# Two-layer pooling/attention decoder trunk on one core: in the feed-forward blocks, the low part of every second weight chunk comes from an accumulating DMA

## The chip, the cores and the metric

The kernel runs on one core of one Trainium2 chip. The metric is the device time of one execution in microseconds (us); lower is better. The kernel before takes 1941.47 us, the median of two runs (1940.99 and 1941.94 us).

A core has TensorE (PE, with its weight loads listed as PEld), VectorE (DVE), ScalarE (ACT), GpSimd (POOL) and SyncE (SP). Each runs its own instructions in the order in which they stand, and they wait for one another through semaphores. SP, ACT and POOL can issue DMAs, which 16 DMA engines carry out.

## The reference

All tensors are float32, for one sequence of 256 tokens with 2048 features. Two layers, each a token mixer and a SwiGLU feed-forward block with 5632 hidden features, each behind an RMS norm and with a residual add:

```
def swiglu(h, wg, wu, wd):
    return (jax.nn.silu(h @ wg) * (h @ wu)) @ wd

for i in range(DEPTH):                      # DEPTH = 2
    hn = rmsnorm(h, norm_mix[i])
    mix = pool_mixer(...) if i % 2 == 0 else diff_attention(...)
    h = h + mix
    h = h + swiglu(rmsnorm(h, norm_ffn[i]), w_gate[i], w_up[i], w_down[i])
return rmsnorm(h, final_norm)
```

`w_gate` and `w_up` are [2048, 5632], `w_down` is [5632, 2048]. The pool mixer of layer 0 multiplies four channel groups by [512, 512] weights and takes causal trailing means; layer 1 is differential attention with `w_qkv` [2048, 6144] and `w_o` [2048, 2048].

## The kernel before

**Three products for one.** A float32 product is carried by float32r operands, which hold 12 significant bits. A weight is split exactly into `wh + wl` and an activation into `xh + xl`. Activations stand feature-major, [128 features, 256 tokens], with `xh` and `xl` side by side. For one *unit*, a [128, 128] block of weights, TensorE runs two matmuls: `big` (line 95) streams [xh | xl], 512 columns, through `wh`, and `small` (line 98) streams `xh`, 256 columns, through `wl`. Both add into one PSUM tile `acc`.

**Chunks.** Weights are read in *chunks* of 8 units, [128, 1024] float32 or 512 KB, by `Stream.unit` (lines 76 to 87). For each chunk SP issues a load into `raw`, ACT copies `raw` to `whi` (the copy rounds, so this is `wh`), and DVE subtracts, `wlo = raw - whi`. `raw`, `whi` and `wlo` have four buffers each, so a chunk can be prepared at most four chunks ahead: the copy into `whi` waits until TensorE is through with the chunk four before.

**The feed-forward block** (lines 270 to 309). Gate and up: 44 output tiles each, in turns, gate 0, up 0, gate 1, up 1 and so on. One output tile has 16 units, two chunks, the first even and the second odd in its stream. Behind each, ACT copies one half of the PSUM tile (`g_c` or `u_c`, line 176), DVE adds the other half and scales, ACT takes the `silu` (line 284) or makes the high part of `h` (line 290). Down: 16 output tiles of 44 units, five and a half chunks each; behind each come two residual adds on DVE (lines 136 and 137, the tile `x_all`), then on ACT the square `sq` (line 131) and the next operand's high part `xg` (line 123). Over both layers the feed-forward has 528 chunks, 352 in gate and up and 176 in down; the other products have 134.

**What sets the order.** A tile framework's scheduler lays out each engine's instructions ahead of time, and so the preparation of a chunk stands about four chunks ahead of its use in the program of ACT, DVE and SP. After that the order on each engine is fixed. POOL does nothing after the start.

Of the kernel before, what the change touches and what calls it, by code (L numbers as in the profile page):

```python
# [17 lines left out]
S = 256  # L18
# [7 lines left out]
CU = 8  # L26
# [10 lines left out]
def trunk_kernel(ctx, tc, x_t, gains, subln, lam_in, band, dist,  # L37
                 pool_w, w_qk, w_v, w_o, w_gate, w_up, w_down, out):
    """Activations are kept feature-major ([feature, token]), so that every product takes
    weights as the stationary operand. A float32 product is carried by three float32r passes:  # L40
    w = wh + wl and x = xh + xl exactly, 12 significant bits each; [xh | xl] stream through wh
    into the halves of one PSUM bank, and xh through wl onto the first half. The norms' row
    scale is applied to the products, which lets them start before it is known."""
    nc = tc.nc
# [8 lines left out]

# [1 line left out]
    gain_sb = const.tile([P, 6, NK], F32, name="gain_sb")  # L55
# [14 lines left out]

# [1 line left out]
    class Stream:  # L72
        def __init__(self, w):
            self.w, self.next, self.have = w, 0, {}

        def unit(self, u):
            c = u // CU
            if c not in self.have:
                raw = wraw.tile([P, CU * P], F32, name="raw")
                nc.sync.dma_start(out=raw, in_=self.w[c])  # L80
                hi = whl.tile([P, CU * P], F32R, name="whi")
                lo = whl.tile([P, CU * P], F32R, name="wlo")
                nc.scalar.copy(hi, raw)  # L83
                nc.vector.tensor_tensor(lo, raw, f32(hi), ALU.subtract)  # L84
                self.have = {c: (hi, lo)}
            hi, lo = self.have[c]
            return hi, lo, (u % CU) * P

    def product(stream, u0, acts):
        """One output tile: units u0.. of the stream against acts; a bank [left | right]."""  # L90
        ps = acc_ps.tile([P, 2, S], F32, name="acc")
        n = len(acts)
        for k, a in enumerate(acts):
            hi, lo, at = stream.unit(u0 + k)
            big = lambda: nc.tensor.matmul(  # L95
                ps.rearrange("p a s -> p (a s)"), hi[:, at:at + P],
                a.rearrange("p a s -> p (a s)"), start=(k == 0), stop=(k == n - 1))
            small = lambda: nc.tensor.matmul(  # L98
                ps[:, 0, :], lo[:, at:at + P], a[:, 0, :], start=False, stop=False)
            if k < n - 1:  # L100
                big()
                small()
            else:
                small()
                big()
        return ps

    def rsqrt(ss, n, cols):
        """(ss / n + eps) ** -0.5 of [128, cols] sums, with one Newton step behind the
        square root's table."""  # L110
        v, s, t, r = (tmp.tile([P, 8], F32, name=f"rs_{x}") for x in "vstr")
        v, s, t, r = v[:, :cols], s[:, :cols], t[:, :cols], r[:, :cols]
        nc.vector.tensor_scalar(v, ss, 1.0 / n, EPS, ALU.mult, ALU.add)
        nc.scalar.activation(s, v, AF.Sqrt)
        nc.vector.reciprocal(s, s)
        nc.vector.tensor_tensor(t, s, s, ALU.mult)
        nc.vector.scalar_tensor_tensor(t, t, -0.5, v, ALU.mult, ALU.mult)
        nc.vector.scalar_tensor_tensor(r, t, 1.5, s, ALU.add, ALU.mult)
        return r

    def split(dst, src, gain):
        """dst = [hi | lo] of src * gain (gain by partition)."""
        nc.scalar.activation(dst[:, 0, :], src, AF.Copy, scale=gain)
# [15 lines left out]
    def token_product(stream, u0, acts):  # L139
        """[tokens, 512] in two banks: acts stationary against 512 columns of the stream."""  # L140
        ps = [acc_ps.tile([P, 512], F32, name="acc") for _ in range(2)]
# [10 lines left out]
    def norm_scale(ssq, rows=True):  # L152
        """Each token's rsqrt(mean square): by partition [128, 2], and [128, S] on every one."""
        ps = aux_ps.tile([P, 512], F32, name="aux")
# [18 lines left out]
    def join(ps, name):  # L173
        """left + right halves of a bank, in SBUF."""
        c = tmp.tile([P, S], F32, name=f"{name}_c", tag="join_c")
# [4 lines left out]

# [1 line left out]
    with tc.tile_pool(name="start", bufs=1, reuse_waits="tile") as st:  # L182
        band_sb = st.tile([P, 4, P + HALO + P], F32, name="band_sb")
        pool_stream = Stream(pool_w)
        nc.scalar.dma_start(out=gain_sb, in_=gains)
        # loads the activation table, and keeps TensorE's clock up, before the data is there
        warm = tmp.tile([P, 8], F32, name="warm")
# [7 lines left out]

        # the first groups' products in plain float32, which wait for no split
        zp = [None] * 4
# [72 lines left out]
    def ffn(layer, ssq, next_gain):  # L270
        """x += swiglu(rmsnorm(x)); prepares the next block's operand and squares."""
        gs, us, ds = Stream(w_gate[layer]), Stream(w_up[layer]), Stream(w_down[layer])
        ssq_next = tmp.tile([P, S], F32, name="ssq")
        with tc.tile_pool(name=f"ffn{layer}", bufs=1, reuse_waits="tile") as hp:
# [17 lines left out]
            for j in range(NK):  # L292
                if j == NK - 1:
                    # has the square root's table in place by the end of the products
                    pre = tmp.tile([P, 8], F32, name="warm")
# [16 lines left out]

# [1 line left out]
    ssq_next = tmp.tile([P, S], F32, name="ssq")  # L314
    with tc.tile_pool(name="attn", bufs=1, reuse_waits="tile") as ap_, \
# [7 lines left out]
        def transpose_probs(h, probs):  # L323
            """aT[h] = [keys, queries] by block of keys."""
            a_t = ap_.tile([P, 2, S], F32, name=f"aT{h}")
# [10 lines left out]
        for h in range(H):  # L336
            # q0 q1 k0 k1
            qk = ap_.tile([P, 4, S], F32, name=f"qk{h}", tag="qk", bufs=8)
            for i in range(4):
# [3 lines left out]
                if r is None:  # L343
# [4 lines left out]
                    nc.vector.tensor_scalar(qs_col, col, QK_SCALE, None, ALU.mult)  # L348
                    # lambda, on all partitions
                    lp = ap_.tile([P, 2], F32, name="lp")  # L350
# [80 lines left out]

# [1 line left out]
    _, r = norm_scale(ssq)  # L433
# [9 lines left out]
def _chunks(w):  # L443
    """[128, columns] -> [chunk, 128, CU * 128], so that each load reads one block of memory."""
    return w.reshape(P, -1, CU * P).transpose(1, 0, 2)


def _units(w):
    """[K, N] -> chunks of [128, N/128 * K/128 * 128]: by column tile, then by row tile."""
    K, N = w.shape  # L450
# [3 lines left out]
def _constants():  # L454
    """What the shapes alone give: the means' bands over tokens, and the distances."""
    import numpy as np
# [57 lines left out]
```

## Time and profile before

| | before |
|---|---|
| median of two runs | 1941.47 us |
| span of the profiled execution | 1939.9 us |
| PE busy | 1923.3 us, 99% |
| DVE busy | 1187.4 us, 61% |
| ACT busy | 938.8 us, 48% |
| POOL busy | 0.7 us |
| share of the span in which the 16 DMA engines carry the SP queue's packets | 59.4% |
| read from HBM | 350.96 MB |
| mean granted TensorE clock | 0.996 |

The span runs from the first to the last instruction; no separate device time of the profiled execution is listed, and the runs' median lies 1.6 us above the span. Matmuls are pipelined, so PE's busy time says that PE had always something to do, not that each matmul is as short as can be. The chain that ended last, followed back from the end, names the work that set the time. In a group of instructions, "idle before" is how long the engine waited ahead of them, and the arrow names what ended that wait.

### The profile page before, as it was taken

The page shows a single profiled execution, that of the slowest core. Times are in us where ns is not written, and L with a number is a line of the kernel's source. Part 1 is how long each engine was busy: PE and PEld are TensorE (multiplying, and loading weights), DVE is VectorE, ACT ScalarE, POOL GpSimd, SP SyncE. Part 2 cuts the span into 40 slices and gives each one's busy share as a digit, 9 for nine tenths or more (in the row PEclk, how much of TensorE's full clock was granted, in tenths as well). Part 3 has the DMA queues.
Part 4 walks back from the last instruction along what each step waited for, and adds up shares of the span by engine and source line. Part 5 has one row for each costly group of instructions (what it writes and reads, how often), then busy time and mean ns, then how long its engine had stood idle before and what let it go on. Part 6 is the DMA issues. An engine that isn't in the chain of part 4 may idle for free.

```text
span 1939.9 us, 27612 instructions
## 1 busy us (share of the span) xinstructions
PE 1923.3 (99%) x10786; PEld 1664.6 (86%) x10786; DVE 1187.4 (61%) x1722; ACT 938.8 (48%) x1379; POOL 0.7 (0%) x6
## 2 busy tenths in 40 slices
PE   9999999999999999999999999999999999999997
PEld 7888888888888888888888888888888888888886
DVE  7766666666655555666655676666666666555554
ACT  7544444454444444544455545454544445444442
POOL 0000000000000000000000000000000000000000
PEclk9999999999999999999999999999999999999999
DMA  6666666656666665555555466665666665666663
GB/s 203 193 186 187 189 184 190 185 184 188 186 190 185 189 190 187 174 174 174 175 178 168 160 188 182 188 185 186 185 189 183 190 187 185 187 190 188 186 188 115
DMA packets 99330, 354.86 MB, mean 183 GB/s; under 512 B 11264, under 2 KB 13568, under 8 KB 99200
## 3 DMA queue, kind: packets, MB, share of 16 engines
q1 hardware_dynamic: 97984, 352.01, 59.4%
q8 instruction: 84, 1.38, 0.3%
q10 hardware_dynamic: 1216, 1.10, 0.2%
q14 instruction: 46, 0.38, 0.1%
HBM read 350.96 MB, written 2.10 MB: 182 GB/s over the span
## 4 chain that ended last, share of the span: by engine, by line
PE 98%; DVE 1%; ACT 0%; DMA 0%; issue 0%; SPq 0%; DVEq 0%
PE acc L95 60%; PE acc L98 30%; PE acc L148 2%; PE acc L149 2%; PE acc L147 2%; PE aux L376 1%; DMA x_all<-x_t 0%; PE aux L419 0%; PE aux L252 0%; DVE y_out L437 0%; PE aux L405 0%; PE aux L251 0%; DVE wlo L84 0%; PE aux L406 0%; PE aux L407 0%; ACT sq_in L227 0%
## 5 line engine op out<-in xcount | busy, mean ns | idle before, releaser
L95 PE MATMUL acc<-xg,whi 128*128 128x512 f32 x3328 | 1164.3, 399 | 0.0
L84 DVE TENSOR_TENSOR wlo<-raw,whi 128x1024 fp32r<-128x1024 f32 x662 | 810.1, 1224 | 475.0 <-ACT whi L83 459.4
L83 ACT CAST whi<-raw 128x1024 fp32r<-128x1024 f32 x662 | 694.7, 1050 | 506.6 <-PE acc L95 436.9
L98 PE MATMUL acc<-xg,wlo 128*128 128x256 f32 x3328 | 902.4, 281 | 0.0
L95 PEld LDWEIGHTS acc<-xg,whi 128*128 128x128 f32 x3328 | 612.6, 188 | 134.2
L98 PEld LDWEIGHTS acc<-xg,wlo 128*128 128x128 f32 x3328 | 628.3, 189 | 20.0
L95 PE MATMUL acc<-h,whi 128*128 128x512 f32 x1408 | 492.1, 394 | 0.0
L98 PE MATMUL acc<-h,wlo 128*128 128x256 f32 x1408 | 390.5, 281 | 0.0
L95 PEld LDWEIGHTS acc<-h,whi 128*128 128x128 f32 x1408 | 262.6, 188 | 59.6
L98 PEld LDWEIGHTS acc<-h,wlo 128*128 128x128 f32 x1408 | 264.0, 188 | 2.9
L176 ACT COPY g_c<-acc 128x256 f32<-128x256 f32 x88 | 32.7, 372 | 166.8 <-PE acc L95 166.8
L176 ACT COPY u_c<-acc 128x256 f32<-128x256 f32 x88 | 32.7, 372 | 166.4 <-PE acc L95 166.4
L178 DVE TENSOR_TENSOR u_s<-acc,u_c 128x256 f32<-128x256 f32 x88 | 37.3, 424 | 92.0 <-ACT u_c L176 92.0
L178 DVE TENSOR_TENSOR g_s<-acc,g_c 128x256 f32<-128x256 f32 x88 | 37.3, 424 | 90.0 <-ACT g_c L176 90.0
L95 PE MATMUL acc<-oT,whi 128*128 128x512 f32 x256 | 89.2, 396 | 0.0
L98 PE MATMUL acc<-oT,wlo 128*128 128x256 f32 x256 | 69.1, 282 | 0.0
L147 PE MATMUL acc<-whi,xg 128*128 128x512 f32 x152 | 60.5, 400 | 2.6 <-ACT whi L83 2.6
L148 PE MATMUL acc<-wlo,xg 128*128 128x512 f32 x152 | 61.7, 406 | 0.7 <-DVE wlo L84 0.7
L149 PE MATMUL acc<-whi,xg 128*128 128x512 f32 x152 | 61.0, 401 | 0.0
L95 PEld LDWEIGHTS acc<-oT,whi 128*128 128x128 f32 x256 | 47.1, 188 | 9.9
L290 ACT CAST h<-h 128x256 fp32r<-128x256 f32 x88 | 35.8, 407 | 39.6 <-DVE h L289 39.6
L98 PEld LDWEIGHTS acc<-oT,wlo 128*128 128x128 f32 x256 | 48.1, 188 | 1.5
(109 smaller groups left out, 751.6 us busy)
## 6 DMA issues: line engine op xcount, KB each, us to landing
raw<-w_gate SPq DMA_DIRECT2D x176, 512.0 KB, 4.1
raw<-w_up SPq DMA_DIRECT2D x176, 512.0 KB, 3.7
raw<-w_down SPq DMA_DIRECT2D x176, 512.0 KB, 4.3
raw<-w_qk SPq DMA_DIRECT2D x64, 512.0 KB, 3.6
raw<-w_v SPq DMA_DIRECT2D x32, 512.0 KB, 3.6
raw<-w_o SPq DMA_DIRECT2D x32, 512.0 KB, 4.3
raw<-pool_w SPq DMA_DIRECT2D x6, 512.0 KB, 7.0
x_all<-x_t SPq DMA_DIRECT2D x3, 512.0 KB, 7.5
```

The lines of the kernel that those rows point to most:

```text
L83: nc.scalar.copy(hi, raw)
L84: nc.vector.tensor_tensor(lo, raw, f32(hi), ALU.subtract)
L95: big = lambda: nc.tensor.matmul(ps.rearrange("p a s -> p (a s)"), hi[:, at:at + P], a.rearrange("p a s -> p (a s)"), start=(k == 0), stop ...
L98: small = lambda: nc.tensor.matmul(ps[:, 0, :], lo[:, at:at + P], a[:, 0, :], start=False, stop=False)
L147: nc.tensor.matmul(ps[t], xh, hi[:, at:at + 512], start=(k == 0), stop=False)
L148: nc.tensor.matmul(ps[t], xh, lo[:, at:at + 512], start=False, stop=False)
L149: nc.tensor.matmul(ps[t], xl, hi[:, at:at + 512], start=False, stop=(k == n - 1))
L176: nc.scalar.copy(c, ps[:, 1, :])
L178: nc.vector.tensor_tensor(s, ps[:, 0, :], c, ALU.add)
L290: nc.scalar.copy(hT[j][:, 0, :], h)
L376: nc.tensor.matmul(sc[:, :nk], qk[:, c, qb * P:(qb + 1) * P], qk[:, 2 + c, :nk], start=True, stop=True)
```

## The change

In the two feed-forward blocks, chunks with an odd number in their stream get `wlo` in another way. ACT writes `-wh` into `wlo`, by a copy of `raw` with scale -1 (it rounds as the copy into `whi` does). Then GpSimd issues a DMA that reads the chunk's weights from HBM a second time and adds them to what stands in `wlo`: `wlo = -wh + w`. DVE's subtraction falls away for these chunks. Even chunks, and all chunks of the other products, are as before. The added DMA has 512 KB, and there are 264 of them. Lines behind the change stand five further down: `big` is line 100 in place of 95, `small` 103 in place of 98.

```
     class Stream:
-        def __init__(self, w):
-            self.w, self.next, self.have = w, 0, {}
+        def __init__(self, w, added=False):
+            self.w, self.added, self.next, self.have = w, added, 0, {}
...
                 nc.scalar.copy(hi, raw)
-                nc.vector.tensor_tensor(lo, raw, f32(hi), ALU.subtract)
+                if self.added and c % 2:
+
+                    nc.scalar.activation(lo, raw, AF.Copy, scale=-1.0)
+                    nc.gpsimd.dma_start(out=lo, in_=self.w[c], accum_op=ALU.add)
+                else:
+                    nc.vector.tensor_tensor(lo, raw, f32(hi), ALU.subtract)
...
-        gs, us, ds = Stream(w_gate[layer]), Stream(w_up[layer]), Stream(w_down[layer])
+        gs, us, ds = Stream(w_gate[layer], True), Stream(w_up[layer], True), Stream(w_down[layer], True)
```

The scheduler places the new instructions. On ACT, in layer 0's gate and up, two output tiles before the change read as follows (`whi` and `raw` are numbered; the even chunk's copy comes first, then the copy of a finished tile's half, then the odd chunk's copy):

```order
L83 CAST whi_2993<-raw_2991 128x1024 [waits DMAHW6_49,PE_49,Activation_49]
L176 COPY g_c_2929<-acc_2884 128x256 [waits PE_49,Activation_49]
L83 CAST whi_3015<-raw_3013 128x1024 [waits DMAHW7_49,Activation_49]
L284 ACTIVATE silu_2934<-g_s_2931 128x256 [waits DVE_49]
L83 CAST whi_3045<-raw_3043 128x1024 [waits DMAHW0_49,PE_49,Activation_49]
L176 COPY u_c_2981<-acc_2936 128x256 [waits PE_49,Activation_49]
L83 CAST whi_3067<-raw_3065 128x1024 [waits DMAHW1_49,Activation_49]
L290 CAST h0_22_512<-h_2986 128x256 [waits DVE_49]
```

And with the change, at the same place in the block:

```order
L83 CAST whi_2931<-raw_2929 128x1024 [waits DMAHW2_49,PE_49,Activation_49]
L86 ACTIVATE wlo_2954<-raw_2951 128x1024 [waits DMAHW3_49,DMASW2_49,PE_49]
L181 COPY g_c_2866<-acc_2820 128x256 [waits PE_49,Activation_49]
L83 CAST whi_2953<-raw_2951 128x1024 [waits Activation_49]
L289 ACTIVATE silu_2871<-g_s_2868 128x256 [waits DVE_49]
L83 CAST whi_2984<-raw_2982 128x1024 [waits DMAHW4_49,PE_49,Activation_49]
L86 ACTIVATE wlo_3007<-raw_3004 128x1024 [waits DMAHW5_49,DMASW3_49,PE_49]
L181 COPY u_c_2919<-acc_2873 128x256 [waits PE_49,Activation_49]
L83 CAST whi_3006<-raw_3004 128x1024 [waits Activation_49]
L295 CAST h0_21_511<-h_2924 128x256 [waits DVE_49]
```

The odd chunk's negated copy (L86) stands ahead of its plain copy (L83) and ahead of the copy of the finished tile's half. It waits for TensorE to be through with the buffer, and the three instructions behind it wait for it.

In the down product of layer 0, ACT's program with the change, around the end of an output tile (`raw_6531` and `raw_6576` belong to odd chunks, `raw_6509`, `raw_6554` and `raw_6599` to even ones):

```order
L83 CAST whi_6511<-raw_6509 128x1024 [waits DMAHW4_49,PE_49,Activation_49]
L83 CAST whi_6533<-raw_6531 128x1024 [waits DMAHW5_49,PE_49,Activation_49]
L86 ACTIVATE wlo_6534<-raw_6531 128x1024 [waits DMASW7_49,PE_49]
L83 CAST whi_6556<-raw_6554 128x1024 [waits DMAHW6_49,DVE_49,PE_49]
L83 CAST whi_6578<-raw_6576 128x1024 [waits DMAHW7_49,PE_49,Activation_49]
L136 ACTIVATE sq_6495<-x_all_87 128x256 [waits DVE_49]
L128 ACTIVATE xg8_96<-x_all_87,gain_sb_76 128x256
L86 ACTIVATE wlo_6579<-raw_6576 128x1024 [waits DMASW0_49,PE_49]
L83 CAST whi_6601<-raw_6599 128x1024 [waits DMAHW0_49,PE_49,Activation_49]
```

Here the plain copy stands first and the negated copy behind it, and for one chunk in this stretch `sq` and `xg`, which wait for the finished tile's residual adds, stand between the two.

POOL's program, which ended with the constants of the start, now goes on with nothing but the accumulating DMAs, each waiting for ACT's negated copy and for the use of its semaphore eight DMAs before (`wlo_560` and so on are the buffers they add to):

```order
L87 DMA wlo_631<-w_up0 128x1024 [waits DVE_49,PE_49,Activation_49]
L87 DMA wlo_686<-w_gate0 128x1024 [waits DMASW0_49,Activation_49]
L87 DMA wlo_739<-w_up0 128x1024 [waits DMASW1_49,Activation_49]
L87 DMA wlo_794<-w_gate0 128x1024 [waits DMASW2_49,Activation_49]
L87 DMA wlo_847<-w_up0 128x1024 [waits DMASW3_49,Activation_49]
```

No other work stands in that queue. TensorE's matmuls keep their order in the feed-forward blocks but for a few rows where the two blocks begin, and SP's loads keep theirs.

## The prediction

> **What bounds the kernel now.** I read the page first, for the shares of the engines and the chain that ended last:
>
> ```profile
> span 1939.9 us, 27612 instructions
> PE 1923.3 (99%) x10786; PEld 1664.6 (86%) x10786; DVE 1187.4 (61%) x1722; ACT 938.8 (48%) x1379; POOL 0.7 (0%) x6
> PE 98%; DVE 1%; ACT 0%; DMA 0%; issue 0%; SPq 0%; DVEq 0%
> L84 DVE TENSOR_TENSOR wlo<-raw,whi 128x1024 fp32r<-128x1024 f32 x662 | 810.1, 1224 | 475.0 <-ACT whi L83 459.4
> L83 ACT CAST whi<-raw 128x1024 fp32r<-128x1024 f32 x662 | 694.7, 1050 | 506.6 <-PE acc L95 436.9
> q1 hardware_dynamic: 97984, 352.01, 59.4%
> ...
> core 0: 1939.9 us, clock 0.996
> ```
>
> TensorE is the bound: 98% of the chain is matmuls, and its clock was all but full (0.996). The preparation of weights is behind a cover: the copies into `whi` spend 436.9 us waiting for TensorE to free a buffer, and the subtractions wait for those copies. So nothing that makes VectorE faster is on the path; the question is only whether the new way of preparing odd chunks stays ahead of TensorE.
>
> How far ahead it has to be, the timeline of ScalarE shows, first in gate and up, then in down:
>
> ```profile
> 401.53 1.05 ACT L83 CAST whi<-raw 128x1024 fp32r<-128x1024 f32 x1 [0.50 <-PE acc L95]
> 404.49 0.37 ACT L176 COPY g_c<-acc 128x256 f32<-128x256 f32 x1 [1.92 <-PE acc L95]
> 404.76 1.05 ACT L83 CAST whi<-raw 128x1024 fp32r<-128x1024 f32 x1
> 405.82 0.42 ACT L284 ACTIVATE silu<-g_s 128x256 f32<-128x256 f32 x1
> 407.18 1.05 ACT L83 CAST whi<-raw 128x1024 fp32r<-128x1024 f32 x1 [0.95 <-PE acc L95]
> 410.15 0.37 ACT L176 COPY u_c<-acc 128x256 f32<-128x256 f32 x1 [1.92 <-PE acc L95]
> ...
> 714.21 1.05 ACT L83 CAST whi<-raw 128x1024 fp32r<-128x1024 f32 x1 [1.78 <-PE acc L95]
> 717.02 1.05 ACT L83 CAST whi<-raw 128x1024 fp32r<-128x1024 f32 x1 [1.77 <-PE acc L95]
> 717.97 0.41 ACT L131 ACTIVATE sq<-x_all 128x256 f32<-128x256 f32 x1
> 718.29 0.49 ACT L123 ACTIVATE xg<-x_all,gain_sb 128x256 fp32r<-128x256 f32 x1
> ```
>
> The copies behind two output tiles start at 404.49 and 410.15: a tile of two chunks takes 5.66 us, a chunk 2.83 (717.02 less 714.21 is 2.81 in down). A buffer freed by TensorE now is used again three chunks later, after 3 x 2.83 = 8.5 us. That is the time in which a chunk must be made ready.
>
> **What the change takes away.** 264 subtractions of 1.224 us, 323 us of VectorE, fall away. They ran beside matmuls, so this is worth nothing by itself; VectorE goes to about 864 us busy.
>
> **What it adds on ScalarE.** 264 negated copies. None is in the trace; the nearest row is the CAST of the same size, 1.05 us, so 277 us, and ScalarE goes to about 1216 us, 63%. In gate and up the negated copy stands ahead of the finished tile's copy: it starts when that tile's last `small` is done, a little before the copy at 404.49, so `g_c`, the odd `whi` and `silu` each come some 0.8 to 1.05 us later. There is room: in the rows above ScalarE idles 1.92 us ahead of each such copy, and the next even chunk's copy only starts 2.4 us after the odd one's (407.18 follows 404.76). `g_c` frees a PSUM tile of which there are five. Price nothing; without the idle time, up to 1.05 us a tile.
>
> **What it adds on SP.** Nothing is issued more. The odd `raw` was freed by a copy and a subtraction, 1.05 + 1.22 us, and is now freed by two copies, 1.05 + 1.05, so loads come no later.
>
> **What it adds on POOL and the DMA engines.** 264 DMAs on a queue that held nothing. TensorE's `small` of the odd chunk now waits for the DMA's landing. From the 8.5 us go, in gate and up, the negated copy, 1.05: the DMA has 7.4 us from issue to landing. In down the plain copy stands first, so 2.1 go: 6.3 us. In eight chunks `sq`, in some `xg` too, stand between the copies and wait for the residual adds: 717.02 to the end of `xg` at 718.78, then 1.05, leaves 8.5 - 2.8 = 5.7 us. Handing over between engines comes on top; in the rows above it does not show as more than a tenth, and I leave it to the spread below.
>
> No accumulating DMA is in the trace, nor any issued by POOL. The rows nearest to it are the loads of the same 512 KB, here all of `raw` and one stretch of it, and the first stretch of the kernel, when the queue was full, beside steady stretches:
>
> ```profile
> DMA to landing us min/median/max: 3.2/3.8/9.6
> DMA to landing us min/median/max: 3.5/4.0/4.5
> ...
> 10.00:20.00 10.00, 6.69 (x17) 3.79 (x16) 9.07 (x13) 8.96 (x17) 0.00 (x0) 0.80 1.02 374
> 200.00:256.00 56.00, 56.00 (x319) 48.59 (x318) 35.81 (x51) 27.81 (x40) 0.00 (x0) 1.00 0.61 186
> ```
>
> (The last three columns of a window are the TensorE clock, the DMA engines' busy share, and GB/s.) From below: an accumulating DMA could land like the fastest load, 3.2 us, if the addition rides along. From above: like the longest load, 9.6 us. I take a load's 4.0, and add that the engine must read two sources, the weights and what stands in `wlo`: another 512 KB at the 374 GB/s of the full queue, 1.4 us. Sharing the engines with one load that is under way half of the time adds 0.7. That gives 6.1 us, nearer to the median load than to the longest, because the queue is 61% busy and not full.
>
> The Trainium skill, DMA: Bandwidth & Descriptors, section Anatomy of one DMA, puts a plain GpSimd-issued DMA at about 2.0 us plus its bytes at 436 GB/s; that would be 3.2 us for 512 KB, an estimate, which matches the fastest load here. With a second read of the same bytes it would be 4.4 us.
>
> With 6.1 us, gate and up have 1.3 us to spare and the down chunks 0.2. The eight late ones lack 0.4; with a spread of half a microsecond around the median (3.5 to 4.5 above) I take 0.6 each, 8 x 0.6 = 5 us, and 2 us for the place where layer 0's block begins and its first odd chunk's copies stand behind the mixer's work. A stall of TensorE counts in full. Sum: 1939.9 + 7 = 1947 us of span; the runs' median lies 1.6 above the span, so 1949.
>
> Do the engines have the capacity? In 5.66 us they now move two loads, 1.05 MB, 186 GB/s. The accumulating DMA adds one read from HBM and one from SBUF; counted as two more loads it makes 2.10 MB, which at 374 GB/s takes 5.61 us. It just fits, and this is the weak point of the forecast.
>
> The Trainium skill, Collectives: The Full Stack, section The bandwidth ceiling, says that an add inside the DMA engine costs no time of its own, but two source reads, at about 31 GB/s for an engine. By it, an estimate, the two loads and the accumulation would take 4.2 us of the 5.66 on 16 engines; no run here shows it yet.
>
> **Rivals.** *The DMA engines become the bound.* The share speaks for it: 186 GB/s at 0.61 busy means 305 GB/s when full, by which 2.10 MB take 6.88 us. Then each of 264 tiles' worth of chunks takes 1.22 us longer, +322 us, 2264 us. If an accumulation costs as much as three loads, 2.62 MB at 374 GB/s are 7.01 us, +1.35 x 264 = +356, 2298 us. It decides from an accumulation that costs more than 2.05 loads. Against it stands the 374 GB/s window, since packets overlap better when many are queued. The page on DMA named above, in Issuing engines are not separate DMA queues, says that all queues share the same 16 engines; with that the share above is the right one to add to.
>
> *The landing is too late, with engines to spare.* One POOL DMA in three steps (descriptors made in software, two reads, a write) may land after 8 us. Buffers then turn over too slowly: each four chunks lose what the landing lacks. At 8.2 us, two loads one behind the other, gate and up lose 88 x 0.8 = 70 us and down 44 x 1.9 = 84: +154, 2096 us. At 9.6 us it is 88 x 2.2 + 44 x 3.3 = 339, 2281 us. From 7.2 us on it costs over 2%. For it: no row shows what POOL's issue costs. Against: steady loads land within 3.5 to 4.5 us.
>
> *Faster, by VectorE's relief.* The subtraction's part of the chain is 0%, and all of VectorE's is 1%, 19 us, most of it at the start and the end, where the change does nothing. At most 2 us: 1939.
>
> That the change does not do what it says can be left out: POOL's program has its 264 DMAs and VectorE's has 264 subtractions fewer.
>
> **How the numbers follow.** Forecast 0.50, its own range 1940 to 1980. The engines as the bound 0.28, the late landing 0.20, faster by anything 0.02. Of the two slower rivals, 0.01 falls to mild cases within 2%. A change of 2%, 39 us, is about what a measurement of this kernel can tell from none: faster by more 0.02, within 0.51, slower by more 0.47. The range begins at 1938, below the gain of 2 us. It ends at 2330, which holds the four prices above; beyond lie accumulations that cost four loads or more, for which I leave 0.13.
>
> **What would show it.** Right: accumulating DMAs land in 5.5 to 7 us, PE stays at 98 to 99% of the span, matmuls in gate and up never wait for a DMA, and a few `small` in down wait 0.3 to 1 us behind `sq`. The DMA share goes to about 0.9. Wrong by the engines: a share of about 1 in gate, up and down alike, and also SP's loads land in 8 us or more. Wrong by the landing: a share well under 0.9, loads still at 4 us, TensorE waiting at each odd chunk, more in down than in gate and up. If the negated copy takes much over 1.05 us, the step on ScalarE is wrong.

## The result, and the profile after

| | before | after |
|---|---|---|
| median of two runs | 1941.47 us | 2049.86 us |
| range of the two | 1940.99 to 1941.94 | 2045.09 to 2054.62 |
| profiled execution, its span | 1939.9 us (span) | 2054.62 us, 2052.7 us |

The ratio is 1.0557, with an interval of 1.0498 to 1.0616: the change costs 108 us. The profiled execution is the longer of the two, so its stages, further down, add up to 113 us more and not 108. This lies inside the range that was forecast and far from the likeliest time, 1949 us.

The page of the kernel after, with the rows that answer to those of before:

```profile
span 2052.7 us, 27976 instructions
...
PE 1953.7 (95%) x10786; PEld 1670.0 (81%) x10786; DVE 885.1 (43%) x1458; ACT 1179.8 (57%) x1643; POOL 228.7 (11%) x270
...
q1 hardware_dynamic: 97984, 352.01, 47.9%
q0 software_dynamic: 38016, 138.43, 39.3%
...
PE 69%; DMA 23%; issue 5%; ACT 2%; DVE 0%; POOL 0%; SPq 0%; ACTq 0%; DVEq 0%; POOLq 0%
...
L89 DVE TENSOR_TENSOR wlo<-raw,whi 128x1024 fp32r<-128x1024 f32 x398 | 487.5, 1225 | 602.7 <-ACT whi L83 592.9
...
L86 ACT ACTIVATE wlo<-raw 128x1024 fp32r<-128x1024 f32 x264 | 279.4, 1058 | 329.3 <-PE acc L103 329.3
...
L87 POOL DMA_DIRECT2D wlo<-w_down x88 | 75.9, 863 | 504.8 <-ACT wlo L86 458.2
...
raw<-w_gate SPq DMA_DIRECT2D x176, 512.0 KB, 5.7
...
raw<-w_down SPq DMA_DIRECT2D x176, 512.0 KB, 6.0
wlo<-w_gate POOLq DMA_DIRECT2D x88, 512.0 KB, 6.3
wlo<-w_up POOLq DMA_DIRECT2D x88, 512.0 KB, 6.0
wlo<-w_down POOLq DMA_DIRECT2D x88, 512.0 KB, 7.9
```

TensorE is no longer the whole chain: 23% of it is DMA. The subtractions went as they should (VectorE 885 us, from 1187), and the negated copy costs what a plain one does (1058 ns). What is new is the DMAs, in the last five rows. The loads now land after 5.7 us in gate and 6.0 in down, and the accumulating DMAs land after 6.3, 6.0 and 7.9 us (medians). The 7.9 belongs to down. On before's page the same loads had landed sooner:

```profile
raw<-w_gate SPq DMA_DIRECT2D x176, 512.0 KB, 4.1
raw<-w_up SPq DMA_DIRECT2D x176, 512.0 KB, 3.7
raw<-w_down SPq DMA_DIRECT2D x176, 512.0 KB, 4.3
```

What TensorE waits for, by cause (us in total, times, longest):

```profile
PEld acc L103 <- DMA wlo<-w_down: 83.2, 66, 3.0
...
PEld acc L103 <- DMA wlo<-w_gate: 16.6, 14, 5.4
...
PEld acc L103 <- DMA wlo<-w_up: 10.0, 8, 2.8
```

These are the weight loads of `small`, which read `wlo`. They wait 83 us in down and 27 us in gate and up, 110 in all: the whole loss. The stretches tell the same (us, then PE, PEld, DVE, ACT, POOL busy, TensorE clock, DMA share, GB/s); the first is gate and up of layer 0, the second down of layer 0, the third gate and up of layer 1. First before, then after:

```profile
200.00:400.00 200.00, 200.00 (x1135) 173.45 (x1134) 127.92 (x177) 98.51 (x142) 0.00 (x0) 1.00 0.62 187
600.00:700.00 100.00, 100.00 (x572) 87.38 (x571) 53.31 (x60) 41.16 (x48) 0.00 (x0) 1.00 0.62 188
1310.00:1560.00 250.00, 250.00 (x1417) 216.82 (x1416) 161.12 (x221) 122.42 (x177) 0.00 (x0) 1.00 0.62 187
```

```profile
200.00:400.00 200.00, 197.22 (x1115) 170.66 (x1114) 86.29 (x137) 127.65 (x175) 29.36 (x34) 1.00 0.99 273
600.00:700.00 100.00, 87.51 (x481) 73.29 (x480) 26.83 (x35) 49.36 (x55) 12.79 (x15) 1.00 0.94 242
1310.00:1560.00 250.00, 249.01 (x1406) 215.08 (x1406) 109.67 (x176) 161.10 (x220) 37.63 (x44) 1.00 1.01 278
```

Two different things have happened. In gate and up the DMA engines are busy all the time (0.99 and 1.01; below, a share near 1 is called full) and TensorE hardly waits. In down they are less full (0.94), move less (242 GB/s), and TensorE does 481 matmuls in 100 us in place of 572, though its clock is 1.00. Something is late there, though the engines still have time to spare.

Cut by the times at which SP issues its loads (the first of `w_down`, the first of `w_qk`, the last of `w_o`, of `w_up` and of `w_down`), the two profiled executions differ so:

| stage | before | after | more |
|---|---|---|---|
| to the end of layer 0's gate and up | 528.2 | 542.1 | 13.9 |
| down, layer 0 | 247.2 | 288.4 | 41.2 |
| attention | 385.5 | 388.2 | 2.7 |
| gate and up, layer 1 | 499.1 | 508.8 | 9.7 |
| down, layer 1 | 246.3 | 288.6 | 42.3 |
| rest | 33.7 | 36.5 | 2.8 |

Down, a third of the chunks, has 83.5 of the 113 us. The timeline of the kernel after shows one turn there, ScalarE's copies for an odd chunk, POOL's issue, and TensorE's first `small` with it:

```profile
644.35 1.05 ACT L83 CAST whi<-raw 128x1024 fp32r<-128x1024 f32 x1 [3.40 <-PE acc L100]
...
645.30 1.05 ACT L86 ACTIVATE wlo<-raw 128x1024 fp32r<-128x1024 f32 x1
...
646.38 0.33 SPq L80 DMA_DIRECT2D raw<-w_down  x1
...
646.65 0.86 POOL L87 DMA_DIRECT2D wlo<-w_down  x1 [6.41 <-ACT wlo L86]
...
654.21 0.39 PE L103 MATMUL acc<-h,wlo 128*128 128x256 f32 x1 [1.05 <-DMA wlo<-w_down]
```

TensorE is through with the old chunk at 644.3. The second copy ends at 646.35 and POOL issues at 646.65, 0.3 us behind it; 7.6 us later the data has landed and TensorE, which has waited 1.05 us, goes on. POOL waited for nothing but the copy. SP issued a load just ahead of it, at 646.38, which will matter below.

### The profile page after: what moved, and what is told of

Read it like the earlier page. It is cut to its first block, busy times and chain, and to the rows that moved or that the text cites. A ratio compares the mean times of both kernels' runs of the same rounds, so it can differ in the third digit from the quotient of the medians.

```text
span 2052.7 us, 27976 instructions
## 1 busy us (share of the span) xinstructions
PE 1953.7 (95%) x10786; PEld 1670.0 (81%) x10786; DVE 885.1 (43%) x1458; ACT 1179.8 (57%) x1643; POOL 228.7 (11%) x270
## 3 DMA queue, kind: packets, MB, share of 16 engines
q1 hardware_dynamic: 97984, 352.01, 47.9%
q0 software_dynamic: 38016, 138.43, 39.3%
q10 hardware_dynamic: 1216, 1.10, 0.2%
## 4 chain that ended last, share of the span: by engine, by line
PE 69%; DMA 23%; issue 5%; ACT 2%; DVE 0%; POOL 0%; SPq 0%; ACTq 0%; DVEq 0%; POOLq 0%
PE acc L100 41%; PE acc L103 22%; DMA wlo<-w_down 15%; DMA wlo<-w_gate 4%; DMA wlo<-w_up 2%; ACT wlo L86 2%; PE acc L153 2%; PE acc L154 2%; PE acc L152 2%; PE aux L381 1%; DMA x_all<-x_t 0%; PE aux L424 0%; DVE y_out L442 0%; PE aux L410 0%; PE aux L411 0%
## 5 line engine op out<-in xcount | busy, mean ns | idle before, releaser
L83 ACT CAST whi<-raw 128x1024 fp32r<-128x1024 f32 x662 | 693.4, 1048 | 381.4 <-PE acc L100 303.0
L89 DVE TENSOR_TENSOR wlo<-raw,whi 128x1024 fp32r<-128x1024 f32 x398 | 487.5, 1225 | 602.7 <-ACT whi L83 592.9
L100 PE MATMUL acc<-h,whi 128*128 128x512 f32 x1408 | 501.0, 398 | 0.0
L86 ACT ACTIVATE wlo<-raw 128x1024 fp32r<-128x1024 f32 x264 | 279.4, 1058 | 329.3 <-PE acc L103 329.3
L103 PE MATMUL acc<-h,wlo 128*128 128x256 f32 x1408 | 400.6, 288 | 62.2 <-DMA wlo<-w_down 61.9
L87 POOL DMA_DIRECT2D wlo<-w_gate x88 | 76.1, 865 | 865.8 <-ACT g_c L181 401.3
L87 POOL DMA_DIRECT2D wlo<-w_down x88 | 75.9, 863 | 504.8 <-ACT wlo L86 458.2
L87 POOL DMA_DIRECT2D wlo<-w_up x88 | 76.0, 864 | 430.9 <-ACT u_c L181 411.1
L141 DVE TENSOR_TENSOR res_t<-acc,x_all 128x256 f32<-128x256 f32 x48 | 20.4, 424 | 104.2 <-PE acc L100 104.2
```

The costliest lines, as they stand in the source:

```text
L86: nc.scalar.activation(lo, raw, AF.Copy, scale=-1.0)
L87: nc.gpsimd.dma_start(out=lo, in_=self.w[c], accum_op=ALU.add)
L100: big = lambda: nc.tensor.matmul(ps.rearrange("p a s -> p (a s)"), hi[:, at:at + P], a.rearrange("p a s -> p (a s)"), start=(k == 0), stop ...
L103: small = lambda: nc.tensor.matmul(ps[:, 0, :], lo[:, at:at + P], a[:, 0, :], start=False, stop=False)
L141: nc.vector.tensor_tensor(t, ps[:, 0, :], x_sb[k], ALU.add)
```

## The theories after the result

*Late landing.* TensorE waits because a buffer comes back too late. What four chunks lose is the landing less the time in hand (7.4 us in gate and up, 6.3 in down). Another buffer, or an earlier issue, would cure it.

*Engines full.* The DMA engines carry what three or more loads weigh, for each pair of chunks, and can't do it in a pair's 5.66 us. Then only less DMA work helps.

*Something else* that the change adds: ScalarE's copies, their order, POOL's issue.

## The experiments

### Without the DMA

```diff
-                    nc.gpsimd.dma_start(out=lo, in_=self.w[c], accum_op=ALU.add)
```

> The negated copies on ScalarE stay, the accumulating DMAs are left out (so the odd chunks' low part is -wh, and the product is another one). Engines-full theory: all of the loss comes with the DMAs, 1940 to 1946 us. Late-landing theory: the same, since the small product then waits only for ScalarE's copy, 1940 to 1946 us. A third theory, that ScalarE's 264 copies and their place ahead of other work cost the time: it stays at 2030 us or more.

Measured: 1940.77 us, a ratio of 0.9998 (0.9988 to 1.0007). ScalarE's 264 copies, their places in its order and VectorE's relief together are worth nothing. The whole loss is the DMA's.

### Gate and up alone, down alone

```diff
-...Stream(w_gate[layer], True), Stream(w_up[layer], True), Stream(w_down[layer], True)
+...Stream(w_gate[layer], True), Stream(w_up[layer], True), Stream(w_down[layer])
```

> The accumulating DMA in gate and up alone, 176 of the 264. Late landing (the copy order of down makes the loss): most of the loss goes, 1950 to 1970 us. Engines full: these products put two thirds of the added bytes on the engines, so two thirds of the loss stays, about 2010 us.

> The accumulating DMA in down alone, 88 of the 264. Late landing: 2015 to 2035 us, the part of the loss that the trace shows in down (about 83 us). Engines full: one third of the loss, about 1978 us.

Measured: 1963.02 us with gate and up alone (1.0114, 1.0088 to 1.0141), +21.6; 2027.88 with down alone (the other way round; 1.0439, 1.0415 to 1.0463), +86.5. The sum is 108.1, the whole loss: the two stages don't touch each other, and what is lost in down isn't a legacy of gate and up. Both times lie where the late landing expected them. With gate and up alone:

```profile
200.00:400.00 200.00, 198.16 (x1121) 171.39 (x1120) 87.13 (x139) 128.59 (x176) 30.23 (x35) 1.00 1.01 276
```

A share of 1.01 with TensorE busy for 198 of 200 us: the loads of a pair of chunks and its accumulation do just about fit.

### A fifth buffer for the low part

```diff
-                lo = whl.tile([P, CU * P], F32R, name="wlo")
+                lo = whl.tile([P, CU * P], F32R, name="wlo", bufs=5)
```

> A fifth buffer for the low parts, nothing else; in down the negated copy then stands ahead of the plain copy. The bytes are the same. Late landing: an odd chunk's DMA may start one chunk (2.83 us) and one copy (1.05 us) earlier against a lack of about 2 us for every four chunks, so down's loss goes: 1945 to 1965 us. Engines full: the bytes still need the engines longer than the matmuls take, 2035 to 2055 us, with a DMA share of 1.0 in down.

Measured: 1974.85 us (1.0184, 1.0159 to 1.0208). The fifth buffer, with the negated copy ahead in down too, takes away 75 of the 108 us. But 33 stay, more than the late landing expected and much less than the rival did:

```profile
200.00:400.00 200.00, 198.88 (x1120) 171.12 (x1118) 87.97 (x141) 132.06 (x176) 30.23 (x35) 1.00 1.02 277
600.00:700.00 100.00, 98.66 (x557) 85.11 (x556) 31.01 (x41) 57.64 (x65) 14.66 (x17) 1.00 1.01 277
```

The landings on its page:

```profile
raw<-w_gate SPq DMA_DIRECT2D x176, 512.0 KB, 7.6
...
raw<-w_down SPq DMA_DIRECT2D x176, 512.0 KB, 7.7
wlo<-w_gate POOLq DMA_DIRECT2D x88, 512.0 KB, 8.5
...
wlo<-w_down POOLq DMA_DIRECT2D x88, 512.0 KB, 8.6
```

Once TensorE asks at its full pace the engines are full in both stages, every transfer lands later (8.5 and 8.6 us for the accumulations), and the fifth buffer covers it, all but some. What stays is lost in the same way as before, in weight loads that wait for an accumulation:

```profile
PEld acc L103 <- DMA wlo<-w_down: 14.3, 24, 1.7
PEld acc L103 <- DMA wlo<-w_gate: 12.8, 15, 6.1
PEld acc L103 <- DMA wlo<-w_up: 8.0, 13, 1.6
```

Those are 35 us, 6.1 of them in one wait. From POOL's issue until TensorE stands ready there are 8.9 us in this kernel (medians of gate, up and down), and the slowest tenth of the DMAs takes 9.1 to 9.3. So the landings are still late, now in their spread; whether full engines make that spread, the next two runs test.

### The same DMA without the addition, with four buffers and with five

```diff
-                    nc.gpsimd.dma_start(out=lo, in_=self.w[c], accum_op=ALU.add)
+                    nc.gpsimd.dma_start(out=lo, in_=self.w[c])
```

> The same DMA from the same queue behind the same copies, but it overwrites wlo with the weights and adds nothing (the low part is then w and not w - wh, another product). Both theories: an accumulated 4 KB row took 328 ns at the median on its engine where a loaded one took 159; if that is the second read, these rows take 159 and the DMAs land in about 5 us, so the time is 1941 to 1955 us. If GpSimd's queue itself is slow, the rows stay near 328 and the time near 2050 us.

> Five buffers for the low parts as in the fourth run, but the DMA overwrites wlo with the weights and adds nothing (another product). If what stayed over with five buffers (33 us) is the DMA engines being full, it goes with the second read, but for the 5 us at the first odd chunk of the blocks: 1941 to 1952 us, DMA share about 0.85. If it is the order of the instructions or the queue of GpSimd, it stays: 1965 to 1980 us.

Measured: 1953.75 us with four buffers (1.0071, 1.0056 to 1.0086), 1946.70 with five (1.0027, 1.0017 to 1.0037), both as expected. Beside the accumulating DMA with five buffers, the plain one saves 28 us, and with it the engines are no longer full. The stretches of the kernel with the plain DMA and five buffers:

```profile
200.00:400.00 200.00, 200.00 (x1134) 173.46 (x1133) 88.84 (x143) 132.66 (x178) 18.92 (x36) 1.00 0.82 278
600.00:700.00 100.00, 100.00 (x573) 87.39 (x572) 32.13 (x42) 58.64 (x67) 9.55 (x18) 1.00 0.82 279
```

And on its page the software queue, which is POOL's: packets, MB, share of the engines' span:

```profile
q0 software_dynamic: 38016, 138.43, 19.6%
```

The same 278 GB/s that filled the engines (1.02) with the addition fill them to 0.82 without it. A row of 4 KB (264 x 128 = 33,792 of them) takes 0.196 x 16 x 1945.6 / 33,792 = 0.181 us here. With the addition, in the kernel with five buffers, it is 0.347 us (its software queue's share is 37.2% of 1970.0). The addition nearly doubles what a row costs its engine, a factor of 1.92.

This agrees with the Trainium skill, Collectives: The Full Stack, section The bandwidth ceiling, which says that the add itself costs nothing and the second source read halves the rate; it tells that of a reduction between cores, and here it holds for an accumulation into the core's own SBUF.

So of the 108 us about 75 go with a fifth buffer, and about 28 more with the second read, that is with half of the accumulation's work on the engines. Both are lost at the same place, in TensorE's wait for the landing. That full engines cause the 28, by late landings, is likely but not shown by itself: a sixth buffer, which would cover a spread and could not help against a lack of capacity, was not run. Some 5 stay even with a plain copy and five buffers.

### The weights from SBUF in place of HBM

```diff
-                    nc.gpsimd.dma_start(out=lo, in_=self.w[c], accum_op=ALU.add)
+                    nc.gpsimd.dma_start(out=lo, in_=raw, accum_op=ALU.add)
```

> The accumulating DMA reads the weights from raw in SBUF and not a second time from HBM; raw is then held until it has landed. If the price is the two reads on the DMA engine, a row still takes about 328 ns; if it is HBM, it falls towards 159. The time: raw is freed 6 to 8 us later with four buffers, so loads come late too, 2150 us or more, by either theory.

Measured, in one run: 2135.14 us, a little under what was expected. Its time says little, since `raw` is now held until the DMA has read it and its next load is late. What it tells is the price of a row:

```profile
q0 software_dynamic: 38016, 138.43, 36.8%
```

0.368 x 16 x 2133.1 / 33,792 is 0.372 us a row, against 0.382 in the kernel after (39.3% of 2052.7). The median packet record of 4 KB is 334 ns against 328. It is not HBM that makes an accumulation dear.

### The copies the other way round

Here the negated copy reads `whi`, so it stands behind the plain copy in gate and up too, as it does in down.

```diff
-                    nc.scalar.activation(lo, raw, AF.Copy, scale=-1.0)
+                    nc.scalar.activation(lo, f32(hi), AF.Copy, scale=-1.0)
```

> The negated copy reads whi in place of raw, so it stands behind the plain copy in gate and up too, as in down. The bytes on the DMA engines are the same. Late landing: gate and up now have 6.3 us for a DMA that landed in 6.3 us at the median before, and more once it collides with the load that the plain copy sets free; they begin to stall as down does (0.95 us a pair of chunks there): 2100 to 2200 us. Engines full: nothing changes, 2040 to 2060 us.

Measured: 2148.63 us (1.106, 1.104 to 1.1079), as the late landing expected. ScalarE's timeline at the end of a tile of gate, with the copies of an odd gate chunk:

```profile
307.20 0.37 ACT L181 COPY g_c<-acc 128x256 f32<-128x256 f32 x1 [2.30 <-PE acc L100]
307.47 1.05 ACT L83 CAST whi<-raw 128x1024 fp32r<-128x1024 f32 x1
308.52 0.42 ACT L289 ACTIVATE silu<-g_s 128x256 f32<-128x256 f32 x1
308.85 1.04 ACT L86 ACTIVATE wlo<-whi 128x1024 fp32r<-128x1024 f32 x1
```

From the freed buffer at 307.2 to the end of the negated copy at 309.9 are 2.7 to 2.8 us, so 5.7 stay in hand of 8.5. The gate DMAs now land after 7.4 us, a microsecond later than before: 1.7 late for each four chunks, 88 x 1.7 = 150 us. By the stages, gate and up lose 145.5. It is the clearest support for the turn of the buffers as the mechanism: no byte was added, and the loss nearly doubled, from 108 to 208 us.

### The negation on VectorE

```diff
-                    nc.scalar.activation(lo, raw, AF.Copy, scale=-1.0)
+                    nc.vector.tensor_scalar(lo, raw, -1.0, None, ALU.mult)
```

> VectorE makes the negated copy from raw, so it waits for no copy on ScalarE; the bytes are the same. Late landing: in down the DMA starts about 1 to 1.5 us earlier against a lack of 1.6 us, so most of down's 84 us goes: 1965 to 2000 us. Engines full: 2040 to 2060 us. If VectorE's copy holds up GpSimd's making of descriptors, POOL's DMA issue takes longer than 0.86 us and the gain is smaller.

Measured: 2042.82 us (1.0531, 1.0509 to 1.0553), a miss for the late landing as it was put. On its page the operation takes 694 ns, so the DMA has some 7.8 us in hand; POOL's issue takes 0.86 us as before, so nothing held it up:

```profile
L86 DVE TENSOR_SCALAR wlo<-raw 128x1024 fp32r<-128x1024 f32 x264 | 183.2, 694 | 199.9 <-PE acc L103 199.7
...
wlo<-w_gate POOLq DMA_DIRECT2D x88, 512.0 KB, 8.1
wlo<-w_up POOLq DMA_DIRECT2D x88, 512.0 KB, 7.6
wlo<-w_down POOLq DMA_DIRECT2D x88, 512.0 KB, 8.3
```

But the DMAs, issued earlier, land later: 8.1 and 7.6 us in gate and up, where they took 6.3 and 6.0. By the stages, down gains 35 us on the kernel after, and gate and up lose 33. The landing isn't a fixed price.

### Half as many accumulations, with four buffers and with five

```diff
-                if self.added and c % 2:
+                if self.added and c % 4 == 3:
```

> Four buffers, and the accumulating DMA for every fourth chunk, 132 in place of 264. If each accumulating DMA costs TensorE its own late landing, half of the loss stays: about 1995 us. If the landing is late because the engines are full, their share falls to about 0.8, the DMAs land in about 6 us and nearly all of the loss goes, not half: 1943 to 1962 us.

> The accumulating DMA for every fourth chunk, as in the run before, with five buffers for the low parts, as in the fourth run. There the engines were 0.78 busy and yet the DMAs landed in 8.6 us, against 7.4 us in hand. If TensorE waits only for late landings, the 2.83 us that a fifth buffer adds cover them, and with the engines not full nothing is left: 1942 to 1955 us. If the DMAs cost the time in another way, 2000 us or more stay.

Measured: 2079.15 us with four buffers (1.0713, 1.0695 to 1.073), slower than twice as many DMAs, which neither theory expected; 1947.57 with five (1.0031, 1.0021 to 1.004), as expected. The four-buffer kernel:

```profile
200.00:400.00 200.00, 188.35 (x1057) 161.44 (x1055) 101.12 (x149) 107.52 (x150) 14.68 (x17) 1.00 0.78 218
600.00:700.00 100.00, 88.67 (x486) 75.70 (x487) 35.17 (x42) 42.90 (x49) 6.90 (x8) 0.98 0.71 198
```

And its waits (us in total, times, longest):

```profile
PEld acc L103 <- DMA wlo<-w_gate: 70.2, 43, 2.7
PEld acc L103 <- DMA wlo<-w_down: 66.4, 41, 2.7
```

The engines are at 0.78 and 0.71, and still its DMAs land after 8.8 us in gate and 7.6 in down. TensorE waits once for nearly each of 44 gate and 44 down DMAs, 1.63 and 1.62 us a time. The landing less the time in hand is 8.8 - 7.4 = 1.4 and 7.6 - 6.3 = 1.3, or 1.6 and 1.6 with the time in hand that the trace shows (7.2 and 6.0 us, see the count below). My expectation had shared the loss out by DMA. But a chain of four buffers loses once in each turn, whether one or two of its four chunks are late together; in down half as many DMAs lose 67 us by the stages, where all of them lose 83.5. With a fifth buffer the landing is still late (8.0 us in gate, 7.8 in down), and the kernel loses 6 us. So DMAs that land late with engines to spare are what rules here, and the mean share is no measure of it.

### All on one queue

```diff
-                nc.sync.dma_start(out=raw, in_=self.w[c])
+                (nc.gpsimd if self.added else nc.sync).dma_start(out=raw, in_=self.w[c])
```

> As the changed kernel, but the feed-forward's loads of raw go through GpSimd's queue too, so loads and accumulating DMAs are served one behind the other and not in turns. If sharing the engines with the loads of another queue makes the landing late, the accumulating DMAs of down land in 5 to 6.5 us in place of 7.9, and the time falls to 1950 to 2010 us. If it is only the sum of the bytes, landing and time stay, 2040 us or more. GpSimd's own issue time is no bound: three DMAs of 0.5 to 0.9 us in 5.66 us.

Measured: 1994.99 us (1.0275, 1.0253 to 1.0298).

```profile
600.00:700.00 100.00, 98.42 (x555) 84.71 (x555) 32.46 (x45) 57.74 (x67) 34.95 (x53) 1.00 0.99 275
```

And the landings on its page:

```profile
wlo<-w_gate POOLq DMA_DIRECT2D x88, 512.0 KB, 7.5
...
wlo<-w_down POOLq DMA_DIRECT2D x88, 512.0 KB, 5.8
```

In down the accumulations now land after 5.8 us, in place of 7.9, though the engines are fuller (0.99), and down loses 6 and 9 us in place of 41 and 42. So a late landing in down does not follow from how much the engines carry; it depends on how the loads and the accumulations are mixed. In gate and up one queue made things worse (7.5 us; 23.5 and 17.4 us lost in the two layers, in place of 13.9 and 9.7). The run changes two things at once, the queue of the loads and their order, behind DMAs that wait for ScalarE, and doesn't say which of them did that.

### What a landing is made of

The trace's packet records give the 128 rows of each accumulation and the rows of loads around them. Medians, in us from POOL's issue to the first row, from the first to the end of the last row, and from there to the landing; beside them how many rows of loads the engines began in the first two of these stretches:

| kernel, DMAs of | to the first row | its rows | to the landing | loads' rows before | loads' rows during |
|---|---|---|---|---|---|
| after, gate | 1.61 | 4.04 | 0.49 | 156 | 103 |
| after, up | 1.61 | 3.90 | 0.49 | 156 | 84 |
| after, down | 2.80 | 4.71 | 0.36 | 174 | 145 |
| every fourth, gate | 1.66 | 6.62 | 0.52 | 101 | 232 |
| every fourth, up | 2.01 | 5.83 | 0.50 | 139 | 270 |
| every fourth, down | 2.80 | 4.66 | 0.33 | 111 | 134 |
| plain copy first, gate | 1.61 | 5.32 | 0.33 | 106 | 156 |
| no addition, five buffers, gate | 2.75 | 1.86 | 0.38 | 120 | 53 |

Its own rows cost 128 x 0.328 / 16 = 2.6 us if the 16 engines do nothing else. Each row of a load that is done among them adds about 0.159 / 16 = 0.01 us: 2.6 + 103 x 0.01 = 3.6 in gate, 2.6 + 145 x 0.01 = 4.1 in down, 2.6 + 232 x 0.01 = 4.9 in gate of the kernel with every fourth chunk, against 4.0, 4.7 and 6.6 measured. The order is right and the size some 0.4 to 1.7 short. So half as many accumulations landed later, and each met 232 rows of loads in place of 103. That is the collision, counted, not explained: a transfer that lasts longer meets more rows, and why more loads ran beside these (35 rows a us in place of 25) is open.

The wait for the first row, 1.6 us in some places and 2.8 in others, doesn't go with the number of rows before it. It goes with the moment of SP's last issue. In the kernel after, SP issues a load 0.2 to 0.5 us ahead of POOL for 75 of the 88 DMAs in down (646.38 and 646.65 in the timeline above), and their first row starts after a median of 2.83 us; the other 13, with SP's last issue more than 1.4 us before, start after 1.58. In gate and up SP's last issue lies about 1.6 us ahead in most cases, and the first row starts after 1.61. With five buffers SP mostly issues within 0.2 us of POOL, and the wait is 3.2 us. The difference of 1.25 us is about what a whole load's rows need on 16 engines, 128 x 0.159 / 16 = 1.27 (an estimate): it looks as if a load that is issued just ahead goes first. This is read from the traces; no run moved SP's issue alone.

### The turn of the buffers, counted

For each kernel the loss by the rule (late in each four chunks, times 88 turns in gate and up, 44 in down or where only every fourth chunk accumulates) beside what the stages show in both layers together, in us:

| kernel, stage | landing | in hand | by the rule | measured | DMA share |
|---|---|---|---|---|---|
| after, down | 7.9 | 6.3 | 70 | 83.5 | 0.94 |
| after, gate and up | 6.3 | 7.4 | 0 | 23.6 | 0.99 |
| every fourth, down | 7.6 | 6.3 | 57 | 67 | 0.71 |
| every fourth, gate and up | 8.8 | 7.4 | 62 | 64.5 | 0.78 |
| plain copy first, gate and up | 7.4 | 5.7 | 150 | 145.5 | 0.94 |
| plain copy first, down | 7.3 | 6.3 | 44 | 61 | 0.95 |
| five buffers, down | 8.6 | 9.1 | 0 | 14.7 | 1.01 |
| one queue, down | 5.8 | 6.3 | 0 | 15.5 | 0.99 |
| one queue, gate and up | 7.5 | 7.4 | 9 | 40.9 | 0.99 |
| negated by VectorE, gate and up | 8.1 | 7.8 | 26 | 56 | 0.99 |
| negated by VectorE, down | 8.3 | 7.8 | 22 | 48 | 0.97 |

Up to a share of 0.95 the rule holds within 17 us. Where the share is above that, 15 to 32 us come on top. (In hand are 8.5 us less the steps between TensorE's release and POOL's issue: 0.7 for VectorE's negation; a fifth buffer adds a chunk, 2.8.)

Two things make the rule come out low. The time in hand, reckoned so, is a little long. From POOL's issue until TensorE stands ready, the traces show 7.2 us in gate and up and 6.0 in down where hardly anything is late (the plain DMA with four buffers), and 8.9 with five buffers: the 0.3 us between the copy's end and POOL's issue is missing from the sum. With 6.0 the three down rows at 7.9, 7.6 and 7.3 us come to 84, 70 and 57, beside 83.5, 67 and 61; in gate and up the fit is no better (70 beside 64.5 for every fourth). And the rule takes medians, where late ones cost time and early ones bring none back: in gate and up of the kernel after, the slowest tenth lands after 7.8 to 8.3 us, and most of the 27 us that TensorE waits there are for those. In all these kernels TensorE's waits for accumulations come to the whole loss of the profiled execution, within 6 us. For the rows with five buffers and for gate and up of the kernel after, the run without the addition makes it likely that the engines' load makes the spread; for the last four rows the split stays open.

## Why the prediction was right or wrong

The median came out at 2049.86 us, between the likeliest case (1949) and rival *The landing is too late* at 8.2 us (2096). It was that rival's mechanism, above all in one of the two stages. The likeliest case failed; what held was the range, wide enough for its rivals' prices.

- **The bound, and VectorE's relief at nothing:** right. Without the DMA the kernel takes 1940.77 us.
- **The steps on ScalarE:** right. The negated copy took 1.058 us (1.05 forecast), and its order costs nothing by itself. ScalarE went to 1179.8 us rather than 1216, since the records of neighbouring copies overlap (644.35 + 1.05 is past 645.30 in the timeline above).
- **SP's loads come no later:** their issue is as forecast, but they land after 5.7 to 6.0 us in place of 3.7 to 4.3. What the change does to others' landing wasn't priced.
- **POOL:** the queue holds nothing else, and it issues 0.3 us behind the end of the negated copy, in gate and up (300.42 and 300.71 us) as in down (646.35 and 646.65); the page names `g_c` and `u_c` as what ended its wait in gate and up, which end at that moment. The issue takes 0.86 us, which had no row before, and lies inside the landing.
- **The landing of 6.1 us: the step that failed.** In gate and up the median was right (6.3 and 6.0), partly by luck: 1.6 us to the first row, 4.0 of rows and 0.5 to the landing are not the terms of the sum. The spread of half a microsecond was too small; the slowest tenth took 7.8 to 8.3, and so gate and up lose 24 us, where nothing but 2 us at the start was forecast. In down the median is 7.9, so the sum of one load, a second read and 0.7 for sharing came out 1.8 us short. By the packet records its own rows need 2.6 us, the loads among them add about 2 in down, and 2.8 pass before the first row. The terms that were too small are the sharing (0.7 was worked out from a load that is under way half of the time, and 145 rows, more than a whole load, were met) and the time before the first row, of which no row of before told, and which was long where SP had just issued a load.
- **The time in hand:** nearly right, 7.2 and 6.0 us by the trace against 7.4 and 6.3. The handing over was put at a tenth at most and takes 0.3. So down had nothing to spare even at 6.1 us, and every tenth above counted 44 times. The rival's own sum at 7.9 us gives 70 us for down; 83.5 was measured.
- **Eight late chunks and the start of the block, 7 us:** the late chunks can't be told apart in a stage that is late all through. At the start of layer 0's block TensorE waits 5.4 us once for `w_gate` (the longest in the row above), where I had taken 2.
- **The capacity, "it just fits":** nearly. Counting an accumulation as two loads was right (0.347 us a row against 0.181; the limit, at 374 GB/s in 5.66 us, is 2.04 loads rather than 2.05). With the landing covered, the engines were full at 1.01 to 1.02 with TensorE 98.7 to 99.4% busy: a pair takes 5.66 / 0.99 = 5.7 us, against 5.61 forecast. That is some 28 us, if the engines' load is its cause, which *The DMA engines become the bound* had priced at 322 or more. The 31 GB/s for an engine that the Trainium skill states (Collectives: The Full Stack, The bandwidth ceiling), from which the prediction had its estimate of 4.2 us, were not reached here: a plain row of 4 KB took its engine 0.181 us, 23 GB/s. The 305 GB/s of that rival came from a share at which a row of a load took 0.214 us (59.4% x 16 x 1939.9 us over 352.01 MB in rows of 4 KB); in the kernel after it took 0.183 (47.9%). The share for a byte isn't constant, so it can't be scaled up to a full engine.
- **What would show it:** of the marks for a late landing, the share under 0.9 didn't come (0.94 in down), and loads didn't stay at 4 us; TensorE waiting in down more than in gate and up did. Of the marks for the forecast, gate and up were to wait for no DMA and waited 22 times. Engines near full and a late landing came together, and the list had them as alternatives.

Of the versions that accumulate, none is faster than the kernel before; half as many accumulations with five buffers (1947.57 us, against 1941.13 beside it) come nearest.

## What to carry to other kernels

A DMA put into a chain of buffers is priced by its landing beside the transfers it will meet, against the time the buffers leave (one less than the buffers, times the chunk time, less the steps in the chain). A forecast that stands on 0.2 us of room in each of 44 turns is a coin toss, so ask first for one more buffer. Look not only at the median of the landing but at its slowest tenth, and at what is issued just ahead of it. Count an accumulating DMA as two loads on its engines, and don't read the mean share as a sign that a single transfer is on time.

## What the runs showed of the hardware

- An accumulating row of 4 KB takes its DMA engine a median of 328 ns, a plain one of the same queue 174, a load 159; its source in SBUF in place of HBM makes no difference (334).
- GpSimd's issue of a DMA of 128 rows takes 0.86 us with the addition and 0.53 without it.
- The landing of the same 512 KB accumulation lay anywhere from 5.8 to 8.8 us (medians of a stage), and half as many of them landed later (8.8 us at a share of 0.78) than all (6.3 at 0.99). How long its own rows take goes with the rows of loads that are done among them (103 rows: 4.0 us, 232 rows: 6.6).
- From POOL's issue to the first row pass 1.6 us in the kernel after where SP's last load was issued more than 1.4 us before, and 2.8 where it was issued 0.2 to 0.5 us before. Why one queue for all helped down and hurt gate and up is open.
